# Rotating 96 images by a quarter turn: a small unread transfer ahead of the loads, one first load in place of two, and a fourth copy on ScalarE

## The chip, the core and the metric

The kernel runs on one core of a Trainium2 chip. Five engines of that core have instruction streams of their own: TensorE (PE, unused here), VectorE (DVE), ScalarE (ACT), GpSimd (POOL) and SyncE (SP), which issues all the transfers. Sixteen DMA engines move the data between the main memory (HBM) and the on-chip memory of 128 partitions (SBUF). The metric is the device time of one execution in microseconds (us), given as the median of several runs.

## The reference

```
def setup_inputs():
    batch, c, h, w = 32, 3, 256, 256
    return {"x": np.random.randn(batch, c, h, w).astype(np.float32)}

def reference(x: np.ndarray) -> np.ndarray:
    return np.rot90(x, k=-1, axes=(-2, -1)).astype(np.float32)
```

Each of the 96 images of 256 x 256 floats is turned clockwise by a quarter. No arithmetic is done: 25.17 MB are read, put in another order, and 25.17 MB are written.

## The kernel before

All rows of all images form one matrix of 24,576 rows of 256 floats. Sixteen rows (R = 16) make a block of 16 KB (E = 4,096 floats), the unit that one partition holds. The blocks are worked on in four groups of 2, 2, 4 and 4 blocks a partition (`sizes`, L49), that is 4, 4, 8 and 8 MB. Each group has one tile (`u0` to `u3`, all shown as `u` in the profile) which stays in place for the whole kernel: it is loaded, turned within itself, and stored from the same bytes.

**Loads.** SP issues them all at the start, one after the other on one queue. Group 0's four megabytes are viewed as four quarters `home[:, 0]` to `home[:, 3]`, each 128 partitions x 2,048 floats, and come in two transfers: the first megabyte of the input goes to quarter 3 (L67), the next three to quarters 0 to 2 (L68). Then follow two transfers for group 1 (L79) and two each for groups 2 and 3 (L42, by the helper `wide`).

**Turning.** VectorE does the turn with 32 x 32 transposes (`turn`, L92), 25 instructions of mostly 128 x 2,048 floats. What a turn writes would in part overwrite what has not been read yet, so ScalarE parks pieces in spare tiles and copies them back (`copy`, L95). There are two spare tiles in PSUM (`spare0`, `spare1`) and two in SBUF (`extra`, `most`). The order of the instructions on each of the two engines is the order of the program: `keep` (L83) ties each instruction to the one before it on its engine.

For group 0, `turn_slab` (L139) handles two slabs of two quarters each, in two turns a slab. The first slab is the input's first and second megabyte; as they lie in quarters 3 and 0, it is named `home[:, ::-3]`, and its two results go to the two PSUM tiles. The second slab is quarters 1 and 2, and its results go to quarters 0 and 3, which are free by then. Three copies on ScalarE end the group (L147 to L149): quarter 0 to quarter 2, `spare1` to quarter 1, `spare0` to quarter 0. The result in quarter 3 already lies where the store takes it from.

Groups 1 to 3 follow with turns and copies of their own (L151 to L193), which the change does not touch. ScalarE's first instruction for them is the copy of a piece of group 2 to `spare1` (L155), so it waits for group 2's loads.

**Stores.** SP issues eight, two for each group, in the order of the groups (L196 to L210). The first is held until a certain ScalarE copy of group 2 has ended (`mark`, L165 and L201), so that stores stand behind the loads; it also waits for group 0's loads. Each later store waits for the turns and copies of its group.

Of the kernel before, what the change touches and what calls it, by code (L numbers as in the profile page):

```python
# [9 lines left out]
def kernel(  # L10
# [14 lines left out]
    nc = tc.nc  # L25
    fp32 = mybir.dt.float32

    B, C, H, W = x.shape
    P = nc.NUM_PARTITIONS
    R = 16  # L30
# [25 lines left out]
    spare = [psum.tile([P, Q], fp32, name=f"spare{h}") for h in range(2)]  # L56
# [4 lines left out]
    def rows_of(rows, n):  # L61
        return rows[first[n] * P * R : (first[n] + sizes[n]) * P * R]


    ld = rows_of(rows_in, 0).rearrange("(b p r) w -> p b (r w)", b=4, p=P)
    home = groups[0].rearrange("p s f -> p (s f)").rearrange("p (b f) -> p b f", b=4)
    nc.sync.dma_start(out=home[:, 3], in_=ld[:, 0])  # L67
    nc.sync.dma_start(out=home[:, :3], in_=ld[:, 1:])  # L68
    for n in range(1, len(sizes)):
        I = sizes[n]  # L70
        ld = rows_of(rows_in, n).rearrange("(a i m r) w -> i m a (r w)", a=2, i=I, m=P // I)
        to = groups[n].rearrange("p s f -> p (s f)").rearrange("p (a f) -> p a f", a=2)
        if I == 4:
            ld = rows_of(rows_in, n).rearrange("(a i m r) w -> a m i (r w)", a=2, i=I, m=P // I)
# [8 lines left out]
    def keep(inst):  # L83

        before = last.get(inst.ins.engine)
        if before is not None:
            tc.add_manual_dep(inst.ins, before, mybir.DependencyInfo(
                mybir.DependencyClass.NoSync, mybir.DependencyReason.SCHED_ONLY), reason="order")
        last[inst.ins.engine] = inst.ins.name

    def turn(out, in_):
        keep(nc.vector.transpose(out=out, in_=in_))  # L92

    def copy(out, in_):
        keep(nc.scalar.copy(out=out, in_=in_))  # L95
# [43 lines left out]
    def turn_slab(src, dsts):  # L139
        s = src.rearrange("p i (r g c) -> p c r g i", r=R // 2, c=R)  # L140
        for h, d in enumerate(dsts):
            d = d.rearrange("p (c k r) -> p c r k", c=hw, r=R // 2)[:, :, ::-1, ::-1]
            turn(out=d, in_=s[:, h * hw : (h + 1) * hw])

    turn_slab(home[:, ::-3], spare)
    turn_slab(home[:, 1:3], [home[:, 0], home[:, 3]])
    copy(out=home[:, 2], in_=home[:, 0])  # L147
    copy(out=home[:, 1], in_=spare[1])
    copy(out=home[:, 0], in_=spare[0])  # L149

    g1, g2, g3 = [Group(n) for n in range(1, 4)]  # L151
    turn_pair(g1, extra)
# [88 lines left out]
```

## Time and profile before

| | us |
|---|---|
| median of 3 runs (122.31 to 122.51) | 122.49 |
| the profiled execution, its own time | 122.36 |
| span of that execution, first to last instruction | 120.6 |
| VectorE busy, 25 instructions | 83.3 |
| ScalarE busy, 22 instructions | 41.9 |
| first transfer issued by SP | 0.73 |
| first turn on VectorE starts | 13.09 |
| last turn on VectorE ends | 96.7 |
| first store issued | 57.99 |

The times of the profile count from the start of the span. An instruction's line is that of the helper that records it, so all turns show L92 and all copies L95. SP's rows show when it issued a transfer and how long the issue took, not the movement of the data, which the profile gives in the DMA rows and, packet by packet, in the trace.

### The profile page before, as it was taken

The numbers are of one execution on the slowest core, as the hardware profiler recorded it, in microseconds if no ns is written. First come the engines' busy times: TensorE is split into PE (matmuls) and PEld (weight loads), VectorE is DVE, ScalarE is ACT, GpSimd is POOL, SyncE is SP. The second block draws the span as 40 slices with busy tenths as digits, with TensorE's granted clock in tenths as the row PEclk, the third lists the DMA queues.
The fourth block names the chain that finished last, engine by engine and source line by source line (L and its number), as shares of the span: only waits on it lengthen the run. The fifth ranks groups of instructions, "written<-read, shape, count | busy, mean of one in ns | idle before, by whom it ended". The sixth has DMA issues, their size and how long they took to land.

```text
span 120.6 us, 124 instructions
## 1 busy us (share of the span) xinstructions
DVE 83.3 (69%) x25; ACT 41.9 (35%) x22; POOL 0.2 (0%) x4
## 2 busy tenths in 40 slices
DVE  0000699999999999999999999999999900000000
ACT  0000400006910099937859389808302900000000
POOL 0000000000000000000000000000000000000000
DMA  3999999998989899999989999999898989898983
GB/s 95 429 427 427 454 429 435 435 500 370 489 380 489 380 435 435 413 457 402 467 370 500 391 478 391 478 391 478 380 489 380 489 380 489 370 500 359 511 359 163
DMA packets 2368, 50.33 MB, mean 417 GB/s; under 512 B 256, under 2 KB 256, under 8 KB 256
## 3 DMA queue, kind: packets, MB, share of 16 engines
q1 hardware_dynamic: 2368, 50.33, 97.4%
HBM read 25.17 MB, written 25.17 MB: 417 GB/s over the span
## 4 chain that ended last, share of the span: by engine, by line
DVE 68%; DMA 10%; issue 2%; SPq 0%; DVEq 0%
DVE u L92 48%; DVE spare L92 13%; DMA u<-in_x_dram 10%; DVE extra L92 5%; DVE most L92 2%; SPq L67 0%; DVEq L92 0%
## 5 line engine op out<-in xcount | busy, mean ns | idle before, releaser
L92 DVE STREAM_TRANSPOSE u<-u 128x2048 f32<-128x2048 f32 x15 | 56.0, 3792 | 0.2
L92 DVE STREAM_TRANSPOSE spare<-u 128x2048 f32<-128x2048 f32 (+1 forms) x4 | 11.7, 2946 | 13.1 <-DMA u<-in_x_dram 13.1
L95 ACT COPY u<-spare 128x2048 f32<-128x2048 f32 (+2 forms) x9 | 13.2, 1518 | 6.7 <-DVE spare L92 3.8
L95 ACT COPY spare<-u 128x2048 f32<-128x2048 f32 x2 | 7.6, 3811 | 8.9 <-DMA u<-in_x_dram 8.8
L95 ACT COPY extra<-u 128x1024 f32<-128x1024 f32 (+1 forms) x3 | 6.4, 2122 | 2.0 <-DMA u<-in_x_dram 2.0
L95 ACT COPY u<-extra 128x1024 f32<-128x1024 f32 (+2 forms) x4 | 6.0, 1670 | 2.7 <-DVE extra L92 2.7
L95 ACT COPY u<-u 128x2048 f32<-128x2048 f32 x1 | 1.9, 1899 | 13.7 <-DVE u L92 13.7
L95 ACT COPY u<-most 128x1792 f32<-128x1792 f32 x1 | 3.3, 3287 | 7.3 <-DVE u L92 7.3
L95 ACT ACT_TABLE_LOAD x1 | 1.3, 1283 | 13.1 <-DMA u<-in_x_dram 13.1
L92 DVE STREAM_TRANSPOSE spare<-spare 128x2048 f32<-128x2048 f32 x2 | 4.6, 2308 | 0.0
L92 DVE STREAM_TRANSPOSE u<-extra 128x2048 f32<-128x2048 f32 x1 | 4.0, 4004 | 0.0
L92 DVE STREAM_TRANSPOSE extra<-u 128x2048 f32<-128x2048 f32 x1 | 3.9, 3895 | 0.0
L95 ACT COPY most<-u 128x1792 f32<-128x1792 f32 x1 | 3.2, 3217 | 0.0
L92 DVE STREAM_TRANSPOSE extra<-extra 128x2048 f32<-128x2048 f32 x1 | 2.3, 2312 | 0.0
L92 DVE STREAM_TRANSPOSE most<-most 128x1792 f32<-128x1792 f32 x1 | 2.0, 1991 | 0.0
L225 POOL MEMSET const-bfloat16-1.0<- 128x1 bf16 x1 | 0.1, 102 | 0.0
L225 POOL MEMSET const-uint8-127<- 128x1 uint8 x1 | 0.1, 102 | 0.0
L225 POOL MEMSET const-float32-0.0<- 128x1 f32 x1 | 0.1, 100 | 0.2 <-issue 0.2
L225 POOL MEMSET const-float32-1.0<- 128x1 f32 x1 | 0.1, 99 | 0.0
## 6 DMA issues: line engine op xcount, KB each, us to landing
u<-in_x_dram SPq DMA_DIRECT2D x4, 4096.0 KB, 43.0
out_dram<-u SPq DMA_DIRECT2D x4, 4096.0 KB, 19.3
out_dram<-u SPq DMA_DIRECT2D x4, 2048.0 KB, 14.7
u<-in_x_dram SPq DMA_DIRECT2D x2, 2048.0 KB, 18.3
u<-in_x_dram SPq DMA_DIRECT2D x1, 3072.0 KB, 11.8
u<-in_x_dram SPq DMA_DIRECT2D x1, 1024.0 KB, 4.8
```

Source lines behind the costliest of these rows:

```text
L92: keep(nc.vector.transpose(out=out, in_=in_))
L95: keep(nc.scalar.copy(out=out, in_=in_))
L225: nc = _bacc.Bacc("TRN2", target_bir_lowering=False, num_devices=1)
```

## The change

```
@@ -64,8 +64,10 @@
     ld = rows_of(rows_in, 0).rearrange("(b p r) w -> p b (r w)", b=4, p=P)
     home = groups[0].rearrange("p s f -> p (s f)").rearrange("p (b f) -> p b f", b=4)
-    nc.sync.dma_start(out=home[:, 3], in_=ld[:, 0])
-    nc.sync.dma_start(out=home[:, :3], in_=ld[:, 1:])
+
+    strip = ctx.enter_context(tc.tile_pool(name="strip", bufs=1)).tile([R, W // 2], fp32, name="strip")
+    nc.sync.dma_start(out=strip, in_=ld[::P // R, 0, : W // 2])
+    nc.sync.dma_start(out=home, in_=ld)
     for n in range(1, len(sizes)):
@@ -142,11 +144,11 @@
-    turn_slab(home[:, ::-3], spare)
-    turn_slab(home[:, 1:3], [home[:, 0], home[:, 3]])
-    copy(out=home[:, 2], in_=home[:, 0])
-    copy(out=home[:, 1], in_=spare[1])
-    copy(out=home[:, 0], in_=spare[0])
+    turn_slab(home[:, :2], spare)
+    turn_slab(home[:, 2:], [home[:, 0], home[:, 1]])
+    for h in range(2):
+        copy(out=home[:, 2 + h], in_=home[:, h])
+        copy(out=home[:, h], in_=spare[h])
```

SP's first transfer is now a small one: 16 half rows of 512 bytes, every eighth partition's first one of the input's first megabyte, go to 16 partitions of a new tile `strip`, which nothing reads. The load of group 0 follows as one transfer of 4 MB, and the input's four megabytes now lie in the quarters in their own order. The number of transfers stays at 16.

The first slab is then quarters 0 and 1, the second quarters 2 and 3, and the second slab's results go to quarters 0 and 1. Neither of them lies where the store takes it from, so ScalarE does four copies: quarter 0 to 2, `spare0` to quarter 0, quarter 1 to 3, `spare1` to quarter 1. VectorE's instructions keep their number, shapes and order; its first turn waits for one transfer in place of two. ScalarE has one copy more. The first store's wait for group 0's loads now takes in the strip's transfer.

## The prediction

> **What bounds the kernel now.** I began with the page's totals and the DMA row of the 40 slices, went on to the DMA queue, then to what SP waited for, and last to short stretches at both ends of the span.
>
> ```profile
> span 120.6 us, 124 instructions
> DVE 83.3 (69%) x25; ACT 41.9 (35%) x22; POOL 0.2 (0%) x4
> ...
> DMA  3999999998989899999989999999898989898983
> ...
> q1 hardware_dynamic: 2368, 50.33, 97.4%
> HBM read 25.17 MB, written 25.17 MB: 417 GB/s over the span
> ```
>
> No slice of the DMA row but the first and the last falls below 8, and the one queue fills 97.4% of 16 engines' span: 117.5 of 120.6 us. The chain of waits names VectorE for 68%, but it ends with the last transpose at 96.7 us. What ends the span is SP waiting for stores:
>
> ```profile
> SPq L236 <- DMA out_dram<-u: 20.9, 3, 9.7
> ```
>
> Twenty us of stores are still queued when the last one is issued, so VectorE and ScalarE have slack and the stream of DMA packets sets the end. In the trace's single packets all 16 DMA engines hold a packet without a gap from 2.7 us to the end; an 8 KB packet takes 0.309 us on one engine (16 engines: 424 GB/s) and a 32 KB one 1.214 us (432 GB/s). All engines carry the same bytes. The 16 completion packets of the first load run at 4.66 to 5.19 us, those of the second at 12.02 to 12.58, the last store's at 118.77 to 119.32: the engines keep the stagger with which they began, and the one that began last ends last. So a change is worth what it does to the start of that engine, as long as the queue never runs dry. The start, in the view of short stretches (us, then width, the engines' busy times, TensorE clock, DMA share, GB/s; a packet counts where it starts, so a share can pass 1):
>
> ```profile
> 1.50:1.75 0.25, 0.00 (x0) 0.00 (x0) 0.00 (x0) 1.00 0.00 0
> 1.75:2.00 0.25, 0.00 (x0) 0.00 (x0) 0.00 (x0) 1.00 1.42 262
> 2.00:2.25 0.25, 0.00 (x0) 0.00 (x0) 0.00 (x0) 1.00 0.37 66
> 2.25:2.50 0.25, 0.00 (x0) 0.00 (x0) 0.00 (x0) 1.00 0.20 66
> 2.50:2.75 0.25, 0.00 (x0) 0.00 (x0) 0.00 (x0) 1.00 0.78 295
> 2.75:3.00 0.25, 0.00 (x0) 0.00 (x0) 0.00 (x0) 1.00 1.03 426
> ```
>
> 262 GB/s over 0.25 us are eight packets of 8 KB, with a mean length of 1.42 x 0.25 x 16 / 8 = 0.71 us against 0.309 later. Eight engines start at 1.77 to 1.96 us and stall; the other eight start at 2.54 to 2.69 and do not (0.31 to 0.38 us each). The latest engine behaves as if it had begun at full pace at 5.19 - 8 x 0.309 = 2.72 us. That figure is what the change can move.
>
> **The change, part by part.**
>
> The strip. SP's sequencer shows the slot that it takes:
>
> ```profile
> 0.73 0.40 SPq L67 DMA_DIRECT2D u<-in_x_dram  x1
> 1.18 0.42 SPq L68 DMA_DIRECT2D u<-in_x_dram  x1
> 1.65 1.38 SPq L79 DMA_DIRECT2D u<-in_x_dram  x2
> 3.07 2.64 SPq L42 DMA_DIRECT2D u<-in_x_dram  x4
> ```
>
> Issue took 0.40 us for 128 pieces and 0.42 for 384, so the count of pieces hardly shows; for the strip's 16 pieces I take the same 0.40 plus the 0.05 between two issues. The first real bytes are then issued at 1.18 and not at 0.73: 0.45 us later. The strip's own packets, 512 bytes on each of 16 engines, are at the pace of the 8 KB packet 0.02 us, and its completion packet is 0.009 us (the 4-byte packets of the trace): 0.03 us an engine, which lies in that 0.45 us. Nothing reads the strip, so nothing waits for it but the first store (below).
>
> The merge. 1 MB and 3 MB become one transfer of the same 8 KB pieces. Bytes, pieces and the number of transfers (16) stay; the issues behind it keep their slots. VectorE waited for both loads and now waits for one that ends with the same byte: it starts with whatever delay the stream has, and its 20 us of cover hold.
>
> What the start really costs is not in the trace: there is no transfer there that meets engines already used but idle. From above: the start as a whole (1.04 us from issue to first packet, the late eight 0.75 us after that) belongs to a big first transfer and moves by the 0.45 us. Below nothing: the strip takes the stall and the stagger upon itself, the load's first packets come at 1.18 + 1.04 = 2.22 us and, at the 0.19 us in which eight engines started, all 16 are at work by some 2.44 to 2.6. That is 0.1 to 0.28 us less than 2.72. I take the upper end, +0.45, because two rows speak for it: the late eight had normal first packets, so what they waited for was not a first use of the engine that a tiny packet would absorb; and the early eight stalled for the same stretch, until about 2.8, which looks like the work of setting up the transfer itself.
>
> ScalarE's fourth copy. It adds one of 1.90 us and reorders three:
>
> ```profile
> 28.05 1.90 ACT L95 COPY u<-u 128x2048 f32<-128x2048 f32 x1 [13.71 <-DVE u L92]
> 29.86 3.63 ACT L95 COPY u<-spare 128x2048 f32<-128x2048 f32 x2
> ...
> 42.30 4.05 ACT L95 COPY spare<-u 128x2048 f32<-128x2048 f32 x1 [8.82 <-DMA u<-in_x_dram]
> ```
>
> Queued behind it is the copy at 42.30 us, which waits 8.82 us for a load; with the extra copy ScalarE is free at 35.4 instead of 33.5, so 6.9 us of idle are left and the price is nothing. If that cover were gone, the copy whose end releases the first store would slip with it: SP waits 44.9 us for ScalarE there and issues at 57.99. The loads' packets run until 60.62 on the first engine; less the 1.04 us from issue to packet that leaves about 1.6 us before the queue would run dry. The 0.45 us moves the loads and that release alike. The turns on VectorE keep count and shapes, their operands only lie in other quarters of the tile: nothing, with the 20 us as cover.
>
> Sum for the profiled execution: 122.36 (span 120.6 and 1.76 around it) + 0.45 + 0 + 0 = 122.81. The median of the runs shown, 122.49, is 0.13 above that execution, so 122.94; I say **122.9 us**, its own range 122.75 to 123.1.
>
> A rule beside this. By the row, the completion packets of the first load at 4.66 to 5.19 us have 16 engines busy on both sides; a completion costs the stream nothing that shows. The Trainium skill, "DMA: Bandwidth & Descriptors", "Anatomy of one DMA", gives each DMA a fixed part of about 2.0 us, most of it the wait until the last byte has landed. The trace agrees that it doesn't hold up the transfers queued behind it; were it exposed ahead of the load, the sum would be 2.0 us more, as an estimate from that page.
>
> **The rivals.**
>
> *The strip hides its slot* (within 0.2%, which is 0.245 us and about what a measurement of this kernel can tell from no change). The stall until 2.5 to 2.8 us is tied to the time since the first request and not to the bytes asked for. For it: the stalled early packets and the late first packets all end at 2.8 to 3.0. Then the load finds the engines ready at about 2.7, as now: -0.15 to +0.2 us, some 122.5.
>
> *The strip pays* (faster). One mechanism: the tiny first transfer takes the late eight's wait, so that they get the load's pieces as early as the others. Place: the first packets of the load on the late engines. Price: up to 0.28 us as above, 122.2. It decides from the point where these start before 2.69 us. For it: a stagger kept to the end means that an even start pays in full. Against: they would have to start within 1.5 us of the load's issue, where the first load took 0.73 to 2.69, nearly 2 us.
>
> *The one transfer starves half the engines* (much slower). If the late eight must wait until the early eight's pieces are made up, 64 pieces took 0.75 us; of the merged load it is 256 pieces, 3.0 us, the latest engine begins 2.2 + 3.0 = 5.2 and not 2.72, and the time is near 125. Against: in turn, the second load's 192 pieces (2.3 us from 3.3 us on, when the first load's were made) would have left the late engines without work between 5.2 and 5.6 us, and the trace has 16 at work there. The Trainium skill, "Perfetto Trace Analysis", "DMA Optimizations", says that transfers split smaller may let some start sooner, which would speak against this merge.
>
> That the change doesn't do what it says: the strip could be left out by the build, as nothing reads it; the built program has it as SP's first transfer, so no chance is kept for that.
>
> **How the numbers follow.** Forecast 0.45; hidden slot 0.30; the strip pays 0.17; starved half 0.08. The forecast lies wholly above +0.2%, the hidden slot within. A strip that pays only 0.1 or 0.2 us ends within 0.2%, so of the 0.17 I leave 0.15 to faster. Slower is 0.45 + 0.08 - 0.01 for a shift that stays just inside: 0.52; the same 0.33. The range leaves out the starved half and the outermost end of the gain: 122.2 to 123.2.
>
> **What would show it.** In the changed kernel's trace: SP issues the strip at 0.73 and the load near 1.18; the first strong stretch of GB/s comes near 2.2 and the full rate near 3.2 instead of 2.75; VectorE's first turn starts near 13.5; ScalarE idles about 6.9 us before the copy that sat at 42.30; from there on all rows are the same, later by one amount. Full rate at 2.75 or before makes me wrong; so does a stretch at half share after 3 us, or a dip where the stores begin near 60 us.

## The result, and the profile after

The changed kernel takes 122.98 us (median of 6 runs, 122.88 to 123.23), the kernel before beside it 122.40 (122.31 to 122.51): a ratio of 1.0049, 95% interval 1.0037 to 1.0062, that is 0.45 to 0.76 us slower. The forecast was 122.9, with 0.45 us for the strip's place in SP's line.

The profiled execution of the changed kernel took 122.91 us. Its page (totals, DMA queue):

```profile
span 121.1 us, 124 instructions
...
DVE 83.6 (69%) x25; ACT 44.0 (36%) x23; POOL 0.2 (0%) x4
...
q1 hardware_dynamic: 2384, 50.34, 97.1%
```

The span is 0.5 us longer. ScalarE has 2.1 us more work in its one copy more, VectorE the same 25 instructions. The queue moved 16 packets more, the strip's, and is as full as before. SP's rows in the timeline (start, length):

```profile
0.72 0.40 SPq L69 DMA_DIRECT2D strip<-in_x_dram  x1
1.19 0.41 SPq L70 DMA_DIRECT2D u<-in_x_dram  x1
1.64 1.38 SPq L81 DMA_DIRECT2D u<-in_x_dram  x2
3.06 2.61 SPq L42 DMA_DIRECT2D u<-in_x_dram  x4
```

The strip takes the place that the first load had, for the same 0.40 us, though it has 16 pieces; the load is issued at 1.19. The start in short stretches (the last two columns are DMA share and GB/s, a packet counts where it starts):

```profile
1.75:2.00 0.25, 0.00 (x0) 0.00 (x0) 0.00 (x0) 1.00 0.14 33
2.00:2.25 0.25, 0.00 (x0) 0.00 (x0) 0.00 (x0) 1.00 0.00 0
2.25:2.50 0.25, 0.00 (x0) 0.00 (x0) 0.00 (x0) 1.00 1.78 295
2.50:2.75 0.25, 0.00 (x0) 0.00 (x0) 0.00 (x0) 1.00 1.14 229
2.75:3.00 0.25, 0.00 (x0) 0.00 (x0) 0.00 (x0) 1.00 0.25 33
3.00:3.25 0.25, 0.00 (x0) 0.00 (x0) 0.00 (x0) 1.00 0.86 295
3.25:3.50 0.25, 0.00 (x0) 0.00 (x0) 0.00 (x0) 1.00 0.79 328
3.50:3.75 0.25, 0.00 (x0) 0.00 (x0) 0.00 (x0) 1.00 1.01 426
```

The 33 GB/s are the strip: all 16 engines start it between 1.77 and 1.95 us, in 0.025 us each, without a stall. Then they stand idle for a quarter of a microsecond. The load's packets come at 2.27, stall (take longer than the same packets do later) as the first load's packets did before: a mean of 0.73 us for the first 16, against 0.309 later. All 16 engines hold a packet from 3.0 us on, and the full rate is there from 3.5, where near 3.2 was forecast. On ScalarE:

```profile
28.57 1.90 ACT L97 COPY u<-u 128x2048 f32<-128x2048 f32 x1 [13.64 <-DVE u L94]
30.50 1.87 ACT L97 COPY u<-spare 128x2048 f32<-128x2048 f32 x1
32.26 1.90 ACT L97 COPY u<-u 128x2048 f32<-128x2048 f32 x1
...
34.20 1.87 ACT L97 COPY u<-spare 128x2048 f32<-128x2048 f32 x1
...
42.89 4.00 ACT L97 COPY spare<-u 128x2048 f32<-128x2048 f32 x1 [6.83 <-DMA u<-in_x_dram]
```

The fourth copy eats two of the 8.82 us in which ScalarE waited for group 2's load, and 6.83 are left.

One number ties start and end together. In the trace's packets the last 8 KB packet of group 0's load ends at 12.58 us before and at 13.09 after; the executions took 122.36 and 122.91. The difference is 109.78 and 109.82 us. What follows the load is the same to 0.04 us, and the whole change lies ahead of it. In these two executions it even lies ahead of the load's first packet: this starts at 1.77 us before and at 2.27 after, and from there to the load's end it is 10.81 and 10.82 us.

### The profile page after: what moved, and what is told of

It reads as the page before. It is cut to its first block, busy times and chain, and to the rows that moved or that the text cites. A ratio compares the mean times of both kernels' runs of the same rounds, so it can differ in the third digit from the quotient of the medians.

```text
span 121.1 us, 124 instructions
## 1 busy us (share of the span) xinstructions
DVE 83.6 (69%) x25; ACT 44.0 (36%) x23; POOL 0.2 (0%) x4
## 4 chain that ended last, share of the span: by engine, by line
DVE 68%; DMA 10%; issue 2%; SPq 0%
DVE u L94 48%; DVE spare L94 13%; DMA u<-in_x_dram 10%; DVE extra L94 5%; DVE most L94 2%; SPq L69 0%
## 5 line engine op out<-in xcount | busy, mean ns | idle before, releaser
L97 ACT COPY u<-u 128x2048 f32<-128x2048 f32 x2 | 3.8, 1902 | 13.6 <-DVE u L94 13.6
```

## The experiments

Two theories stood against each other. **Slot**: the strip costs its 0.45 us place in SP's line, and the rest is free. **Merge**: part of the 0.58 us belongs to the merged load or the fourth copy. A third, **paid back**, had the strip help the start and hide part of a dearer merge. In the table, "load ends" is the end of the last 8 KB packet of the profiled execution, and "own time" that execution's time. The edits below are against the changed kernel, that of the strip alone against the kernel before; lines that make, resize or drop the tile `strip` are left out save in one, and the last four kernels of the text have no strip.

| kernel | median us | ratio to before, 95% interval | load ends | own time | difference |
|---|---|---|---|---|---|
| before | 122.40 | | 12.58 | 122.36 | 109.78 |
| changed | 122.98 | 1.0049, 1.0037 to 1.0062 | 13.09 | 122.91 | 109.82 |
| no strip | 122.59 | 1.0011, 1.0002 to 1.0020 | 12.71 | 122.53 | 109.82 |
| strip, 1 + 3 MB | 122.90 | 1.0033, 1.0020 to 1.0045 | 13.08 | 122.94 | 109.86 |
| strip second | 122.64 | 1.0014, 1.0005 to 1.0023 | 12.82 | 122.64 | 109.82 |
| two strips | 123.42 | 1.0077, 1.0064 to 1.0090 | 13.44 | 123.42 | 109.98 |
| 1 + 3 MB, four copies | 122.40 | 0.9996, 0.9987 to 1.0005 | 12.64 | 122.47 | 109.83 |
| strip by ScalarE | 122.53 | 1.0010, 1.0002 to 1.0019 | 12.72 | 122.51 | 109.79 |
| strip of 128 pieces | 123.08 | 1.0056, 1.0042 to 1.0070 | 13.63 | 123.40 | 109.77 |
| 0.5 + 0.5 + 3 MB | 123.30 | 1.0072, 1.0060 to 1.0085 | 13.46 | 123.26 | 109.80 |
| cut at partition 16 | 131.67 | 1.0756, 1.0742 to 1.0771 | 21.32 | 131.61 | 110.29 |
| halves, two issuers | 130.75 | 1.0678, 1.0663 to 1.0693 | 20.47 | 130.73 | 110.26 |

**No strip.** The changed kernel without its first transfer:

```
-    nc.sync.dma_start(out=strip, in_=ld[::P // R, 0, : W // 2])
     nc.sync.dma_start(out=home, in_=ld)
```

> The merged 4 MB load and the four copies stay, the strip is gone. Theory 'slot' (the strip costs its 0.45 us place in SP's line and the rest is free): as the kernel before, 122.4 us within 0.15; full DMA rate from about 2.75 us. Rival 'merge' (part of the 0.58 us belongs to the merged load or the fourth copy): 122.5 to 122.7, the last engine's first completion of the load later than 12.58 us. Rival 'paid back' (the strip evens the start and gives back part of a dearer merge): 122.7 or more.

122.59. Most of the loss goes with the strip, which costs 122.98 - 122.59 = 0.39 us, but not all: the interval lies above the kernel before, by 0.02 to 0.24 us. Slot alone is not enough.

**The strip alone,** ahead of the two loads and three copies of before:

```
+    nc.sync.dma_start(out=strip, in_=ld[::P // R, 0, : W // 2])
     nc.sync.dma_start(out=home[:, 3], in_=ld[:, 0])
     nc.sync.dma_start(out=home[:, :3], in_=ld[:, 1:])
```

> The kernel before with the strip alone in front: 1 MB, 3 MB and three copies stay. Slot: 122.4 + 0.45 to 0.55 = 122.85 to 122.95, no more than the changed kernel. Merge: 122.85 and clearly below the changed kernel's 122.98. Paid back: below 122.8, as the strip's help is there without the merge.

122.90, 0.46 us above the 122.44 beside it: the place in the line. The theory that the strip pays back falls: it asked for less than 122.8 here and for 122.7 or more without a strip, where 122.59 was measured. A help of less than 0.1 us is not excluded, as the strip cost 0.39 us ahead of one load and 0.46 ahead of two. The load's first packets, at 2.22 us, stall even longer behind it (a mean of 1.06 us for the first 16).

**The strip second,** the same transfer behind the load:

```
-    nc.sync.dma_start(out=strip, in_=ld[::P // R, 0, : W // 2])
     nc.sync.dma_start(out=home, in_=ld)
+    nc.sync.dma_start(out=strip, in_=ld[::P // R, 0, : W // 2])
```

> The changed kernel with the strip issued right behind the 4 MB load. Slot: the engines have work when its place in the line comes, so the 0.45 us is covered: 122.4, as without a strip, plus some 0.03 us for its packets. If the transfer itself and not its place costs (packets, completion, another semaphore): 122.9 to 123.0, as in the changed kernel.

122.64, against 122.59 without a strip. The transfer costs next to nothing where the engines have work when its place comes.

**Two strips,** the suspected cost doubled:

```
+    nc.sync.dma_start(out=strip[:R], in_=ld[::P // R, 0, : W // 2])
+    nc.sync.dma_start(out=strip[R:], in_=ld[::P // R, 0, : W // 2])
```

> Two strips (the same 16 half rows twice, to two sets of 16 partitions) ahead of the 4 MB load. Slot: a second place in the line, 122.98 + 0.45 = 123.4, the load issued near 1.63 us and its first packet near 2.7. If the first small transfer is what costs (a start paid once): 123.0.

123.42, another 0.44 us. SP's rows show the second place:

```profile
0.72 0.38 SPq L69 DMA_DIRECT2D strip<-in_x_dram  x1
1.17 0.41 SPq L70 DMA_DIRECT2D strip<-in_x_dram  x1
1.61 0.42 SPq L71 DMA_DIRECT2D u<-in_x_dram  x1
```

The load's first packet starts at 2.72 us, 1.11 after its issue. The cost is paid for each place and not once.

**The strip by ScalarE,** so that SP's line is free of it:

```
-    nc.sync.dma_start(out=strip, in_=ld[::P // R, 0, : W // 2])
+    nc.scalar.dma_start(out=strip, in_=ld[::P // R, 0, : W // 2])
```

> The changed kernel with the strip issued by ScalarE, so that it takes no place in SP's line. Slot: SP issues the load at 0.73 us and the time is that of the merged load without a strip, 122.6. If the two issuers share what makes the pieces up, the load is delayed all the same: up to 123.0. If a strip that costs no slot helps the start: below 122.5.

122.53, the time without a strip. Both engines issue at once:

```profile
0.72 0.43 ACTq L69 DMA_DIRECT2D strip<-in_x_dram  x1
0.73 0.43 SPq L70 DMA_DIRECT2D u<-in_x_dram  x1
```

The same bytes, packets and completions as in the changed kernel, and 0.45 us less with the load back at 0.73. The time is that without a strip (1.0010 with it, 1.0011 without). But the strip no longer goes ahead of the load. It has a queue of its own, and its packets run at 3.14 to 3.46 us, behind the load's first at 1.83. The changed kernel, then this one (KB, us from issue to landing):

```profile
strip<-in_x_dram SPq DMA_DIRECT2D x1, 8.0 KB, 1.5
strip<-in_x_dram ACTq DMA_DIRECT2D x1, 8.0 KB, 3.4
```

So this run shows that the transfer costs nothing without SP's place, and nothing about whether a strip ahead of the load helps. The Trainium skill, "DMA: Bandwidth & Descriptors", "Issuing engines are not separate DMA queues", says that issuing from several engines saves only the issuer's time; the trace agrees, and here that time is the whole 0.45 us.

**A strip of 128 pieces** on 128 partitions, one place with eight times the packets:

```
-    ... .tile([R, W // 2], fp32, name="strip")
-    nc.sync.dma_start(out=strip, in_=ld[::P // R, 0, : W // 2])
+    ... .tile([P, W // 2], fp32, name="strip")
+    nc.sync.dma_start(out=strip, in_=ld[:, 0, : W // 2])
```

> The changed kernel with a strip of 128 half rows on 128 partitions, eight pieces of 512 bytes on each engine in place of one. Slot: SP's place is 0.40 + 0.05 us whatever stands in it, and the eight small packets (8 x 0.025 us, as the strip's packets measured) are over before the load's come: 123.0, as with 16 half rows. If the pieces count: 123.2 or more, the load's first packet later than 2.27 us.

123.08, 0.1 us above 16 pieces, with intervals that overlap widely, and the load's first packet at 2.28 us against 2.27: the place sets the cost here too. The profiled execution was the longest of the five, so its load's end is late for the kernel.

**1 + 3 MB with four copies** asks where the 0.13 to 0.19 us of the runs without a slot belong:

```
-    nc.sync.dma_start(out=home, in_=ld)
+    nc.sync.dma_start(out=home[:, 0], in_=ld[:, 0])
+    nc.sync.dma_start(out=home[:, 1:], in_=ld[:, 1:])
```

> No strip, four copies as in the changed kernel, but the first 4 MB again as 1 MB and 3 MB (quarter 0, then quarters 1 to 3). The merged load without a strip measured 122.59. If the merged load is what costs its 0.15 us: 122.4, first packet at 1.77 us. If the fourth copy or the other order of copies costs: 122.6.

122.40, 0.13 us under the strip by ScalarE in the same series (11 runs each, 122.28 to 122.54 against 122.45 to 122.73). So the fourth copy is free and the merged load costs. The traces show half of it: from SP's issue to the first packet it is 1.03 to 1.05 us where the first bulk transfer is 1 MB (before, this kernel, strip with 1 + 3 MB), and 1.08 to 1.12 us where it is 4 MB (six kernels). The load's end is 12.64 against 12.71 and 12.72. The other half is not resolved in single executions.

**0.5 + 0.5 + 3 MB,** to see whether a still smaller first transfer starts better:

```
-    nc.sync.dma_start(out=home, in_=ld)
+    nc.sync.dma_start(out=home[:, 0, : Q // 2], in_=ld[:, 0, : Q // 2])
+    nc.sync.dma_start(out=home[:, 0, Q // 2 :], in_=ld[:, 0, Q // 2 :])
+    nc.sync.dma_start(out=home[:, 1:], in_=ld[:, 1:])
```

> No strip, four copies; the 4 MB load as 0.5, 0.5 and 3 MB (pieces of 4, 4 and 8 KB). If a place in SP's line costs only where the engines have nothing to do: 0.5 MB is 1.2 us of work against 0.45 us, so 122.4, as with 1 and 3 MB. If a smaller first transfer also shortens the stall of the first packets: 122.0 to 122.3. If each transfer costs by itself: 122.8.

123.30, 0.5 us above the dearest branch, so none of them holds. The packets begin at 1.75 us and from 2.6 on hardly an engine is idle, but from 3.0 to 3.7 there is a second stall: 4 KB packets, 0.159 us in the steady part, take 0.3 to 0.5. It leaves the engines' last completion packets of the load 0.96 us apart, against 0.43 with 1 + 3 MB, and the last engine at 13.46. Smaller pieces as such explain little: 16 an engine at 0.159 in place of 8 at 0.309 make 0.07 us. What brings the second stall stays open.

**Two cuts by partitions,** the first to see whether four pieces an engine start sooner, the second to let two issuers share the load:

```
-    nc.sync.dma_start(out=home, in_=ld)
+    nc.sync.dma_start(out=home[:R], in_=ld[:R])
+    nc.sync.dma_start(out=home[R:], in_=ld[R:])
```

> No strip; the 4 MB load is cut by partitions, first 16 partitions (4 pieces of 8 KB on each of 16 engines), then the other 112. If a first transfer with fewer pieces starts sooner and that is what the merged load lost: first packet at 1.77 us, no gap before the second transfer's pieces (4 x 0.309 = 1.24 us of work against 0.45 us), 122.3 to 122.45. If the stall of the first packets is the same whatever the first transfer is and only its place in the line counts: 122.4 to 122.6.

```
-    nc.sync.dma_start(out=home, in_=ld)
+    nc.sync.dma_start(out=home[:64], in_=ld[:64])
+    nc.scalar.dma_start(out=home[64:], in_=ld[64:])
```

> No strip; partitions 0 to 63 of the 4 MB load are issued by SP and 64 to 127 by ScalarE at the same time. Slot: both halves start where the merged load did, all behind is issued no later: 122.4 to 122.6. If making up the pieces of the merged load is what delays its first packet (1.84 us against 1.77): two issuers share it, 122.3 to 122.4.

131.67 and 130.75: both far off all that was expected. The load of group 0 runs at half pace, and the later ones at full. First the cut at partition 16, then the halves:

```profile
5.00:10.00 5.00, 0.00 (x0) 0.00 (x0) 0.00 (x0) 1.00 0.97 195
10.00:15.00 5.00, 0.00 (x0) 0.00 (x0) 0.00 (x0) 1.00 1.01 283
...
25.00:30.00 5.00, 4.97 (x3) 0.00 (x0) 0.00 (x0) 1.00 1.02 436
```

```profile
5.00:10.00 5.00, 0.00 (x0) 0.00 (x0) 0.00 (x0) 1.00 1.01 236
10.00:15.00 5.00, 0.00 (x0) 0.00 (x0) 0.00 (x0) 1.00 1.00 244
...
25.00:30.00 5.00, 4.97 (x3) 0.00 (x0) 0.00 (x0) 1.00 1.02 433
```

The DMA share is full in every stretch while the rate is half: the engines hold a packet all the time, but an 8 KB packet takes 0.59 and 0.53 us (medians from 6 to 11 us) in place of 0.309. A share of 1.0 says that the engines are occupied and not that they move data at their pace. Of the first packets they say this much: with four pieces on each engine the first one came 1.01 us after the issue, against 1.03 to 1.05 with eight and 1.08 to 1.12 with 32; with two issuers it came after 1.49, and each issue took about 0.7 us and not 0.4. Whether a sooner packet would have saved time, these two cannot tell.

## Why the prediction was right, and where its reasons were not

**The strip's place: right.** 0.45 us were forecast from SP's rows; the strip cost 0.39 (against none), 0.44 (a second one), 0.45 (against ScalarE's issue) and 0.46 us (ahead of two loads) by the medians, 0.34 to 0.48 us by the ratios to before.

**The merge: priced at nothing, measured at 0.13 to 0.19 us** (by the ratios 1.0010 to 1.0014 against 0.9996, 0.17 to 0.22 us). "Bytes, pieces and the number of transfers (16) stay" was true, but the first bulk transfer now has 32 pieces on each engine and not 8, and its first packet comes some 0.07 us later after the issue. With it the sum closes: the strip's 0.46 us ahead of two loads and the 0.15 us of the merged load above the kernel beside it (122.59 against 122.44) make 0.61, and 0.58 was measured. This is the term that was mis-sized. The difference that was forecast, 0.45 us, is the low end of the measured interval, 0.45 to 0.76. That the forecast of 122.9 came within 0.08 of 122.98 is in part luck: it started from 122.49, the median of three runs, and the six runs of the result give 122.40 for the kernel before, so that 0.09 us too much at the start made up for most of the missing term.

**The choice of the upper end: right, for a reason that does not hold.** The prediction built on eight late engines that "had normal first packets". In the changed kernel the seven engines that begin last, at 2.55 to 2.71 us, took 0.50 to 0.91 us for their first packet of the load. And with the same first megabyte as before, in the kernel with four copies, no engine was late:

```profile
1.75:2.00 0.25, 0.00 (x0) 0.00 (x0) 0.00 (x0) 1.00 4.10 524
2.00:2.25 0.25, 0.00 (x0) 0.00 (x0) 0.00 (x0) 1.00 0.00 0
2.25:2.50 0.25, 0.00 (x0) 0.00 (x0) 0.00 (x0) 1.00 0.36 66
2.50:2.75 0.25, 0.00 (x0) 0.00 (x0) 0.00 (x0) 1.00 0.00 0
2.75:3.00 0.25, 0.00 (x0) 0.00 (x0) 0.00 (x0) 1.00 0.70 295
3.00:3.25 0.25, 0.00 (x0) 0.00 (x0) 0.00 (x0) 1.00 1.00 426
```

524 GB/s are 16 packets: all 16 engines begin by 2.00 us, stall for about 1.0 us together, and end up where the other pattern did (12.64 against 12.58). What holds across the kernels is that the first 16 packets of 8 KB take 0.58 to 1.06 us in the mean and not 0.309, whether small packets went ahead (changed, strip with 1 + 3 MB, two strips) or not. So the start as a whole moved with the load, as the argument from above said, and the strip ahead of it took no stall away. Each kernel was traced once, so whether eight late engines belong to the kernel before or to that one execution stays open. Why the first packets stall, no run shows.

**The rivals.** A slot hidden by a stall tied to the time since the first request is refuted by the second strip, which added its full 0.44 us. A strip that pays is refuted by the two pairs in which it goes ahead of the load: it made the time 0.39 and 0.46 us longer. ScalarE's issue cannot test this, as its strip came behind the load's first packets. Half the engines starved did not happen: all 16 have packets from 3.0 us on, and the whole loss is 0.58 us.

**The covers: right.** ScalarE's fourth copy cost nothing: 122.40 with it and two loads. VectorE started at 13.60 (forecast near 13.5) and the idle time before the copy of group 2 is 6.83 (6.9). The first store was issued at 58.67, still 2.5 us before the first engine was through with the loads at 61.20, and all 16 engines hold a packet throughout. The rows behind the load are not later by one amount, as was forecast: the first turn by 0.51 us, the copy of group 2 by 0.59, the first store by 0.68. As the queue stays full, this costs nothing.

**The 2.0 us beside the sum.** The Trainium skill, "DMA: Bandwidth & Descriptors", "Anatomy of one DMA", gives its fixed part of about 2.0 us for transfers issued by GpSimd. Here SP issues, and from the strip's issue to its landing it was 1.5 us in all. None of it held up the load behind the strip, whose first packet came 1.08 us after its own issue, against 1.11 without a strip.

**Splits.** The Trainium skill, "Perfetto Trace Analysis", "DMA Optimizations", says that smaller transfers may let some start sooner. In the first packet both splits here agree: 1.76 us with 1 + 3 MB and 1.75 with 0.5 + 0.5 + 3 MB, against 1.84 with one load. In the time they differ: the first took 0.13 us less than one load with the strip by ScalarE, the second 0.7 us more than one load without a strip.

No version here beats the kernel before; the nearest, 1 + 3 MB with four copies, equals it.

## What to carry to other kernels

Where one queue is busy from the first byte to the last, look at when the first load ends on the last DMA engine: here the time was that end + 109.8 to 110.0 us through every variant of the whole-width load. When the last engine begins does not settle it, as the first packets stall: all began by 1.96 us with 1 + 3 MB and four copies, eight only from 2.54 in the kernel before, and the load ended at 12.64 and 12.58. A small transfer at the head of the line cost its issue slot, about 0.45 us, with 16 pieces of 512 bytes and much the same with 128; behind the first load, or from another issuer, the same transfer cost nothing that could be measured. A start pattern seen in one execution should not carry an argument until a second trace shows it.

## What the runs showed of the hardware

Cutting a load by adjacent partitions (16 and 112, or 64 and 64 from two issuers) halved its pace: 8 KB packets took 0.59 and 0.53 us in place of 0.309, at 195 to 283 GB/s in place of 423 to 441, while loads of every second partition (group 1's, 64 of 128) kept the full pace in the same executions (0.615 us for 16 KB, 0.611 in the kernel before). That the cut and not the size is to blame is suggested by group 1's loads, of 2 MB as well, and not shown by a run of its own.

Sixteen pieces of 512 bytes, one to an engine, started 1.05 us after their issue by SP and landed 1.5 us after it, with no stall; the first 16 packets of 8 KB on idle engines took 0.58 to 1.06 us in the mean, 1.9 to 3.4 times their steady 0.309, in each kernel with a whole-width load in such pieces.

The engines keep the stagger with which they end the first load: its completion packets lie at 12.60 to 13.09 us in the changed kernel, those of the last store at 119.36 to 119.86.
